# A decoder layer on one core: modulation's third row moved to the vector engine, output projection split in contiguous halves, steps reordered

## The chip, the core and the metric

The kernel runs one hybrid decoder layer in float32 on one core of a Trainium2 chip. The core has a matrix engine (TensorE, in the profile PE, with its weight loads shown apart as PEld), a vector engine (DVE), a scalar engine (ACT), GpSimd (POOL), and SyncE (SP), whose queue here issues nearly all DMAs. The metric is the device time of one execution in microseconds. The kernel before takes 797.26 us, the median of three runs (797.19 to 798.94).

## What is computed

The input is a sequence of 256 tokens with 1024 channels, `x`, and one conditioning vector `c`. Cut to what matters here:

```python
mod = silu(c) @ ada_w + ada_b                      # 6 x 1024 numbers: sh1 sc1 gt1 sh2 sc2 gt2
xn   = rmsnorm(x) * (1 + sc1) + sh1
proj = xn @ w_in                                   # q, kv latent, indexer, rwkv columns, gate_a, gate_r
o_attn = sparse attention (indexer scores, top 64 keys of each query)
o_rwkv = rwkv-7 state recurrence over the sequence
merged = sigmoid(gate_a) * (o_attn @ w_branch_attn) + sigmoid(gate_r) * (o_rwkv @ w_branch_rwkv)
h  = x + gt1 * (merged @ w_out)                    # output projection
xn2 = rmsnorm(h) * (1 + sc2) + sh2
out = h + gt2 * (top-2-of-32 expert SwiGLU MLPs of xn2)
```

All weights, those of all 32 experts included (192 loads of 1 MB), are read from HBM.

## The kernel before, in words

The program has two parts. The front part runs from the first load to the router: modulation, input projection, rwkv, indexer and attention, gates, branches, output projection, router. The second part streams the expert weights through SBUF and multiplies them with the tokens that chose them.

**The modulation.** `ada_w` has 1024 rows and 6144 columns. The kernel treats its result as three rows of 2048 numbers. Row 0 (sh1, sc1) is made first, since everything needs it. Rows 1 and 2 (gt1, sh2, sc2, gt2) are needed only at the output projection and later. They are made by `modulation()`: a row has eight k-parts, each a 1 MB load of 128 by 2048, and `mod_part` (L403 to L407) multiplies it on TensorE: a stationary of 32 columns that all hold the silu of c, and four moving tiles of 512 columns, so that row piece g lands on partitions 32g to 32g+31 of one PSUM bank (line L406). Each float32 matmul leaves two records in the trace, so a k-part has eight.

**Split products.** Products that must be exact use `split` (L510): a 128x512 weight tile w is written as h (w rounded to the engine's short float) and l = w - h, and `mm3` (L528) makes three matmuls, h by x_h, h by x_l, l by x_h (L530, L531, L532). The first letter of a split's code says who makes h (A: ACT at L519, P: POOL at L517), the second who makes l (D: DVE, P: POOL, both at L520). `SPLIT` holds four codes for each stage, taken in turn. There are four pairs of buffers, used round and round.

**The output projection** (L1495 to L1517) works on `w_out` in four loads of two k each. The 1024 output columns are split into eight blocks, and block m takes columns m, m+8, m+16, .... So the split reads the weights with a stride of 8 elements and packs four blocks (128 columns each) into a 128x512 tile; a k has two such tiles, each followed by its 12 matmuls of 128x128 by 128x256. The weight tile that TensorE loads is contiguous.

**The order of the work.** The front part is written as five generators (rwkv, selection, attn, gate, mod), and the string `ORDER` says which of them takes the next step (a letter each). `LORD` gives the order of the weight loads on SP's queue. Loads go into an arena, and are issued as soon as there is room; `RESERVE` holds back part of the arena at each stage. The compiler's scheduler then orders the instructions of an engine; what an engine's row holds at the end is shown below for the places of interest.

Names that the text uses: the X-solve is the 15-step forward substitution of the rwkv chunk (L858 multiply, L859 reduce, on DVE), closed by `diagonal_blocks` (L897, L898) and the copy L905; the latent's norm is an inverse square root in steps of 128x2 on DVE (L360 to L369), and the indexer's small transposes (L1086) and score products (L1101) follow it on TensorE.

Of the kernel before, what the change touches and what calls it, by code (L numbers as in the profile page):

```python
# [57 lines left out]
FORCE0 = True
WIDE = 'a'
_S = ("AD", "PD", "AP", "PD")  # L60
SPLIT = (('PD', 'PD', 'AP', 'AD'), ('PD', 'PD', 'AP', 'PD'), ('PP', 'PP', 'AD', 'AD'), ('AD', 'AP', 'AD', 'AD'), ('AD', 'PD', 'AP', 'PD'))
PRIO = ('mod', 'sel', 'rwkv', 'attn', 'gate')
ORDER = 'rrrrrrmrrmmrrmrrmrrrrrrmrrrmmmrrmrmmmmrsrmaarmrmarrramrmamrrmraarrmmaarmarmaasrmmasaasmmsrarssrasraaarrarrarraasrssasssararasgrssssgraargrsrgsrsgggsrrsmgmmgsmrrrrggrgrgrrggggrsaggrrrggrgrrrgagagaggggaaaagggggaaaggaagggagagggaggaaaaagaggaaaaaggaaaaaaaggaggggggggggg'
LORD = (0, 1, 2, 3, 4, 5, 6, 7, 8, 9, 10, 12, 13, 15, 11, 14, 17, 16, 18, 23, 19, 20, 21, 22, 24, 28, 25, 27, 26, 29, 30, 31, 32, 33, 34, 35, 36, 37, 38, 44, 40, 39, 41, 42, 51, 45, 43, 47, 48, 52, 50, 46, 49)
INFO = []
QUADS = NE // 4
ENDS = ((0, 512), (512, 512))
# [90 lines left out]
def layer_kernel(tc, I, out, dbg=None):  # L158
    nc = tc.nc
    dbg = dbg or (lambda name, ap: None)  # L160
    ALL = CFG[2]
    TOT = ALL - 6144 - 1024 * NP2
    RING = CFG[0] * 4096
    ctxs = []

# [1175 lines left out]

    def modulation():
        rows = []
        i = 0
        for r in (1, 2):
            row = load_adab(r)
            ps = PS()
            for k in range(8):
                yield ("ada", r, k)
                mod_part(ps, r, k, k == 0, k == 7)  # L1350
                if k < 7:
                    yield 1.5
            nc.vector.tensor_add(row, row, ps)
            rows.append(row)
            yield 1.5
# [99 lines left out]
    del pairs[NPO:]  # L1455
# [497 lines left out]
```

## Time and profile before

| | before |
|---|---|
| median of 3 runs | 797.26 us |
| profiled execution | 798.72 us, its span 796.8 us (1.9 outside the span) |
| PE busy | 676.4 us (85%), 4657 instructions |
| DVE / ACT / POOL busy | 285.3 / 167.6 / 144.2 us |
| DMA | 261.38 MB, mean 328 GB/s over the span |
| mean granted TensorE clock | 0.948 of full speed |

The rows of the section further down are whole lines of views of this execution. In a list of groups by line, a row gives line, engine, operation, output<-input (partitions x elements, type), count | busy us, mean ns of one | idle time of the engine ahead of them, and who ended it. In a timeline a row gives start, length, engine, line, operation and count; in brackets stands the idle time before it and who ended it.

### The profile page before, as it was taken

How to read it: one execution, taken by the hardware profiler on the slowest of the kernel's cores; microseconds unless marked ns; L12 is line 12 of the kernel's file. 1: busy time of each engine (PE TensorE's matmuls, PEld its weight loads, DVE VectorE, ACT ScalarE, POOL GpSimd, SP SyncE). 2: the span in 40 equal slices, each digit the busy share in tenths (PEclk: the TensorE clock that was granted, in tenths of full speed). 3: DMA queues.
4: the chain of work that ended last, by engine and by line, in shares of the span. 5: the costliest groups of instructions: out<-in, count | busy, mean ns of one | idle time of the engine just before them, and what ended most of it. 6: DMA issues, size and time to landing. Idle time of an engine off the chain costs nothing.

```text
span 796.8 us, 11470 instructions
## 1 busy us (share of the span) xinstructions
PE 676.4 (85%) x4657; PEld 364.7 (46%) x4657; DVE 285.3 (36%) x665; ACT 167.6 (21%) x347; POOL 144.2 (18%) x176
## 2 busy tenths in 40 slices
PE   5897989799998998889999778878768868878667
PEld 2785657468888877853342312312312312312112
DVE  2577789697336557741210160100100100100001
ACT  2445412144156644321110100100100100000000
POOL 1446744331314117610000000000000000000000
PEclk9899999899999999989999899899999999899889
DMA  9997467443656456779999999999999999999994
GB/s 333 389 308 253 165 221 282 146 154 105 218 208 239 133 178 246 292 257 420 422 421 422 421 420 422 421 420 423 420 421 422 420 421 422 420 421 422 422 392 180
DMA packets 63590, 261.38 MB, mean 328 GB/s; under 512 B 7952, under 2 KB 19216, under 8 KB 38448
## 3 DMA queue, kind: packets, MB, share of 16 engines
q1 hardware_dynamic: 63248, 260.11, 83.4%
q8 instruction: 37, 0.61, 0.3%
q10 hardware_dynamic: 288, 0.52, 0.2%
q14 instruction: 17, 0.14, 0.0%
HBM read 259.57 MB, written 1.05 MB: 327 GB/s over the span
## 4 chain that ended last, share of the span: by engine, by line
DMA 46%; PE 10%; DVE 3%; SPq 1%; issue 1%; POOL 1%; ACT 0%; POOLq 0%; DVEq 0%
DMA arena<-in_expert_w_down_dram 17%; DMA arena<-in_expert_w_gate_dram 13%; DMA arena<-in_expert_w_up_dram 12%; DMA more<-in_expert_w_gate_dram 2%; DMA more<-in_expert_w_up_dram 2%; PE ps_e L1626 2%; DVE split L520 1%; PE ps_e L1611 1%; SPq L288 1%; PE ps_e L1660 1%; PE acc L1701 1%; PE acc L1708 1%; PE ps_e L1653 1%; PE ps_e L1632 0%; PE ps_r L1471 0%
## 5 line engine op out<-in xcount | busy, mean ns | idle before, releaser
L1626 PE MATMUL ps_e<-arena,more 128*32 128x512 f32 x440 | 87.6, 656 | 23.9 <-DMA arena<-in_expert_w_gate_dram 12.0
L1626 PE MATMUL ps_e<-arena 128*32 128x512 f32 x416 | 82.4, 682 | 20.4 <-DMA arena<-in_expert_w_gate_dram 11.7
L1653 PE MATMUL ps_e<-arena 128*32 128x512 f32 x360 | 84.3, 609 | 13.5 <-DMA arena<-in_expert_w_down_dram 9.6
L520 DVE TENSOR_TENSOR split<-arena,split 128x512 fp32r<-128x512 f32 x77 | 70.7, 928 | 45.6 <-ACT split L519 31.8
L1637 ACT ACTIVATE arena<-ps_e 128x512 f32<-128x512 f32 x8 | 4.8, 597 | 244.8 <-PE ps_e L1626 244.8
L1638 DVE SCALAR_TENSOR_TENSOR arena<-arena,ps_e 128x512 f32<-128x512 f32 x8 | 5.5, 688 | 140.2 <-ACT arena L1637 140.2
L1691 POOL TENSOR_TENSOR arena<-arena 128x256 f32<-128x256 f32 x8 | 4.9, 615 | 280.7 <-PE ps_e L1694 279.0
L1670 DVE TENSOR_TENSOR arena<-ps_e,more 128x512 f32<-128x512 f32 (+1 forms) x17 | 11.8, 691 | 122.2 <-PE ps_e L1653 109.1
L519 ACT CAST split<-arena 128x512 fp32r<-128x512 f32 x66 | 45.0, 688 | 48.1 <-PE ps_g L531 30.3
L520 POOL TENSOR_TENSOR split<-arena,split 128x512 fp32r<-128x512 f32 x33 | 47.2, 1431 | 42.6 <-ACT split L519 27.8
L564 PE MATMUL ps_a<-split 128*128 128x256 f32 x360 | 52.1, 304 | 3.1 <-ACT split L476 1.9
L1626 PEld LDWEIGHTS ps_e<-arena,more 128*32 128x32 f32 x440 | 19.4, 118 | 76.3 <-issue 30.9
L564 PEld LDWEIGHTS ps_a<-split 128*128 128x128 f32 x360 | 47.9, 205 | 12.1 <-issue 6.5
L1626 PEld LDWEIGHTS ps_e<-arena 128*32 128x32 f32 x416 | 17.8, 122 | 74.0 <-issue 35.8
L517 POOL TENSOR_SCALAR split<-arena 128x512 fp32r<-128x512 f32 x44 | 36.9, 842 | 70.2 <-PE ps_g L531 18.7
L1653 PEld LDWEIGHTS ps_e<-arena 128*32 128x32 f32 x360 | 19.6, 110 | 64.3 <-issue 31.2
L530 PE MATMUL ps_g<-split 128*128 128x256 f32 x128 | 39.1, 306 | 0.0
L532 PE MATMUL ps_g<-split 128*128 128x256 f32 x128 | 36.9, 289 | 2.0 <-POOL split L520 2.0
L1639 DVE SCALAR_TENSOR_TENSOR arena<-arena,ps_e 128x512 f32<-128x512 f32 x8 | 8.2, 1029 | 82.5 <-PE ps_e L1626 82.5
L531 PE MATMUL ps_g<-split 128*128 128x256 f32 x128 | 36.8, 288 | 0.0
L1611 PEld LDWEIGHTS ps_e<-arena,more 128*128 128x128 f32 x256 | 30.7, 195 | 13.2 <-issue 8.2
L532 PE MATMUL ps_a<-split 128*128 128x256 f32 (+1 forms) x96 | 30.4, 317 | 6.2 <-DVE split L520 6.2
(378 smaller groups left out, 1192.5 us busy)
## 6 DMA issues: line engine op xcount, KB each, us to landing
arena<-in_expert_w_gate_dram SPq DMA_DIRECT2D x54, 1024.0 KB, 19.8
arena<-in_expert_w_up_dram SPq DMA_DIRECT2D x53, 1024.0 KB, 19.8
arena<-in_expert_w_down_dram SPq DMA_DIRECT2D x53, 1024.0 KB, 19.8
arena<-in_w_in_dram SPq DMA_DIRECT2D x18, 1024.0 KB, 7.8
arena<-in_ada_w_dram SPq DMA_DIRECT2D x16, 1024.0 KB, 6.1
more<-in_expert_w_up_dram SPq DMA_DIRECT2D x11, 1024.0 KB, 19.8
more<-in_expert_w_down_dram SPq DMA_DIRECT2D x11, 1024.0 KB, 19.8
arena<-in_ada_w_dram SPq DMA_DIRECT2D x16, 512.0 KB, 10.9
```

Source lines behind the costliest of these rows:

```text
L517: nc.gpsimd.tensor_scalar(h, w, 1.0, 0.0, op0=OP.mult, op1=OP.add)
L519: nc.scalar.copy(h, w)
L520: (nc.gpsimd if p[1] == "P" else nc.vector).tensor_sub(l, w, h.bitcast(F32))
L530: nc.tensor.matmul(ps, l[0], r[0], start=start, stop=False)
L531: nc.tensor.matmul(ps, l[0], r[1], start=False, stop=False)
L532: nc.tensor.matmul(ps, l[1], r[0], start=False, stop=stop)
L564: nc.tensor.matmul(p, a[:, kk, :], b[:, 4 * hf + kk, :], start=(i == 0 and kk == KORD[0]), stop=(i == 2 and kk == KORD[-1]))
L1611: nc.tensor.matmul(ps[:, n * kk:n * kk + n], h2[:, a, 2 * k2 + kk, :], oh(a), start=(a == 0), stop=(a == 1))
L1626: nc.tensor.matmul(ps[32 * g:32 * g + 32, :], xg[:, 4 * i + k, 32 * g:32 * g + 32], w[:, k, :], start=(i == 0 and k == 0), stop=(i == 1 an ...
L1639: nc.vector.scalar_tensor_tensor(hidb[0:r].rearrange("p (j q) -> p q j", j=4), thb[0:r].rearrange("p (q j) -> p q j", j=4), 0.5, psu[0:r, ...
L1653: nc.tensor.matmul(pss[c][32 * g:32 * g + 32, :], hTb[:, 2 * i + j, 32 * g:32 * g + 32], w[:, j, 512 * c:512 * c + 512], start=(i == 0 and ...
L1670: nc.vector.tensor_mul(Yb[0:r, c:c + 512], ps[0:r], gt2[0][0:r, g:g + 512])
```

## The change

Five things change. Line numbers after the first edit fall by one or two.

1. Modulation row 2 (sc2 and gt2) leaves TensorE, but for its last step. A tile `acc` of 128x2048 collects, over the eight k-parts, the weights times the k-th column of silu(c): ACT writes the first, DVE adds the others by scalar_tensor_tensor (four of 128x512 for each k-part). Then four matmuls with a stationary of ones sum over the partitions.
2. The output projection splits contiguous halves of 512 columns into one of two wide buffers (two halves of 1024 columns, in the same memory as the four pairs), and runs the eight blocks of a k once both halves are split. TensorE now takes its stationary tile with a stride of 8 elements. One `SPLIT` code changes there, AP to PP.
3. In stages 1 and 2 the `SPLIT` codes change too: one POOL subtraction goes to DVE, one POOL copy goes to ACT.
4. `ORDER`, `LORD` and `RESERVE` are other tables. Row 2's loads go behind gate, branch and output weights in the load order.
5. The last copies, `leave`, no longer share a tile between DVE and ACT: DVE copies 512 columns.

```diff
-RESERVE = (29696, 12288, 15360, 4096, 0)
+RESERVE = (29696, 16384, 18432, 4096, 0)
-SPLIT = (..., ('PD', 'PD', 'AP', 'PD'), ('PP', 'PP', 'AD', 'AD'), ('AD', 'AP', 'AD', 'AD'), ('AD', 'PD', 'AP', 'PD'))
+SPLIT = (..., ('PD', 'PD', 'AP', 'AD'), ('AP', 'PP', 'AD', 'AD'), ('AD', 'AP', 'AD', 'AD'), ('AD', 'PD', 'PP', 'PD'))
...
-    pairs = [(b.get(512), b.get(512)) for b in [B] * NPO + [B2] * (NP2 - NPO)]
+    wide = [(B.get(1024), B.get(1024)) for _ in range(2)]
+    pairs = [tuple(t[:, 512 * i:512 * i + 512] for t in p) for p in wide for i in range(2)]
...
+        acc = M(2048)
+        for k in range(8):
+            yield ("ada", 2, k)
+            w = need(("ada", 2, k))[:, 0]
+            for q in range(4):
+                s = slice(512 * q, 512 * q + 512)
+                if k == 0:
+                    nc.scalar.mul(acc[:, s], w[:, s], csb[:, k, 0:1])
+                else:
+                    nc.vector.scalar_tensor_tensor(acc[:, s], w[:, s], csb[:, k, 0:1], acc[:, s], op0=OP.mult, op1=OP.add)
+                if q == 1:
+                    yield 0.0, 1.0
+            done(("ada", 2, k))
+            yield 0.0, 1.0
+        row = load_adab(2)
+        ps = PS()
+        for g in range(4):
+            nc.tensor.matmul(ps[32 * g:32 * g + 32, :], ones[:, 0:32], acc[:, 512 * g:512 * g + 512], start=True, stop=True)
+        nc.vector.tensor_add(row, row, ps)
...
-    def out_part(m, k, w, i):
-        mm3(block(m), (w[0][:, i, :], w[1][:, i, :]), (mh[:, k, :], ml[:, k, :]), k == 0 and m > 5,
+    def out_part(m, k, w):
+        mm3(block(m), (w[0][:, m:1024:8], w[1][:, m:1024:8]), (mh[:, k, :], ml[:, k, :]), k == 0 and m > 5,
...
+    cnt_split[0] += cnt_split[0] % 2
     for j in range(4):
         w = need(("wo", j))
-        ws = {}
-        for hh, kk in ((0, 0), (0, 1), (1, 0), (1, 1)) if j == 3 else ((0, 0), (1, 0), (0, 1), (1, 1)):
-            ws[hh, kk] = split(w[:, kk, :].rearrange("p (c k) -> p k c", k=8)[:, 4 * hh:4 * hh + 4, :])
...
+        ws = []
+        for kk in range(2):
+            ws.append(wide[cnt_split[0] // 2 % 2])
+            for hh in range(2):
+                split(w[:, kk:kk + 1, 512 * hh:512 * hh + 512])
+            if j < 3:
+                for m in range(8):
+                    out_part(m, 2 * j + kk, ws[kk])
+                continue
...
-            if a == 0:
-                nc.scalar.copy(y[:, a, c:c + 512], o)
-            else:
-                nc.vector.tensor_copy(y[:, a, c:c + 256], o[:, 0:256])
-                nc.scalar.copy(y[:, a, c + 256:c + 512], o[:, 256:512])
+            (nc.vector.tensor_copy if a else nc.scalar.copy)(y[:, a, c:c + 512], acc[2 * a + c // 512])
```

What the engines' rows look like at three places. First DVE at the end of the X-solve, before: L858 and L859 are the solve's last step, L905, L897 and L898 its closing, L815 a copy of rwkv scores, L520 a split, and L360 the first step of the latent's norm.

```order
177 L858 TENSOR_TENSOR arena<-arena 128x450
178 L520 TENSOR_TENSOR split<-arena,split 128x512
179 L859 TENSOR_REDUCE arena<-arena 128x2x15
180 L905 COPY arena<-arena 128x512
181 L897 STREAM_TRANSPOSE arena<-arena 128x512
182 L898 TENSOR_TENSOR arena<-arena 128x1024
183 L815 TENSOR_SCALAR arena<-ps_r 64x4x64
184 L360 TENSOR_SCALAR arena<-ps_a 128x2
```

The same place on DVE, after: L857 and L858 are now the solve, L896 and L897 the closing, L358 the norm's first step, L360 its second, L363 its third, and L1363 the new additions of row 2.

```order
174 L1363 SCALAR_TENSOR_TENSOR arena<-arena 128x512
175 L858 TENSOR_REDUCE arena<-arena 128x2x13
176 L358 TENSOR_SCALAR arena<-ps_a 128x2
177 L857 TENSOR_TENSOR arena<-arena 128x392
178 L814 TENSOR_SCALAR arena<-ps_r 64x4x64
179 L858 TENSOR_REDUCE arena<-arena 128x2x14
180 L814 TENSOR_SCALAR arena<-ps_r 64x4x64
181 L857 TENSOR_TENSOR arena<-arena 128x450
182 L360 TENSOR_SCALAR arena<-arena 128x2
183 L1086 COPY arena<-ps_a 128x16
184 L858 TENSOR_REDUCE arena<-arena 128x2x15
185 L363 TENSOR_TENSOR arena<-arena 128x2
```

The norm's steps and the indexer's copy now stand within the solve's last steps, ahead of its closing, which stands some 15 rows further down; two additions of row 2 stand within the solve.

Second, DVE after, behind the solve: the additions of row 2 (L1363) among the state's copies (L934), the indexer's score sums (L1108) and the splits (L519).

```order
283 L1363 SCALAR_TENSOR_TENSOR arena<-arena 128x512
284 L1108 SCALAR_TENSOR_TENSOR arena<-arena 128x256
285 L1363 SCALAR_TENSOR_TENSOR arena<-arena 128x512
286 L1108 SCALAR_TENSOR_TENSOR arena<-arena 128x256
287 L1363 SCALAR_TENSOR_TENSOR arena<-arena 128x512 x2
288 L1108 SCALAR_TENSOR_TENSOR arena<-arena 128x256
289 L934 COPY arena<-ps_r 128x256
290 L1108 SCALAR_TENSOR_TENSOR arena<-arena 128x256
291 L519 TENSOR_TENSOR split<-arena,split 128x512
292 L1363 SCALAR_TENSOR_TENSOR arena<-arena 128x512
```

Five additions stand ahead of the split in row 291; in the kernel before none stands there.

Third, POOL in the output projection, before (L517 makes h of a P split, L520 the l of an AP split):

```order
122 L517 TENSOR_SCALAR split<-arena 128x512
123 L520 TENSOR_TENSOR split<-arena,split 128x512
124 L517 TENSOR_SCALAR split<-arena 128x512 x2
125 L520 TENSOR_TENSOR split<-arena,split 128x512
126 L517 TENSOR_SCALAR split<-arena 128x512 x2
127 L520 TENSOR_TENSOR split<-arena,split 128x512
128 L517 TENSOR_SCALAR split<-arena 128x512 x2
```

and after (L516 makes h, L519 the l of the PP split):

```order
112 L516 TENSOR_SCALAR split<-arena 128x512
113 L1322 TENSOR_TENSOR arena<-arena 128x512
114 L516 TENSOR_SCALAR split<-arena 128x512 x3
115 L519 TENSOR_TENSOR split<-arena,split 128x512
116 L516 TENSOR_SCALAR split<-arena 128x512 x3
117 L519 TENSOR_TENSOR split<-arena,split 128x512
118 L516 TENSOR_SCALAR split<-arena 128x512 x3
119 L519 TENSOR_TENSOR split<-arena,split 128x512
```

For two k, POOL had two h and one l, and has three h and one l; the l stands behind both h of its own k.

## Rows read from the trace of the kernel before

**Rows 1.** Chain that ended last, some of its 304 pieces: start, length, what.

```profile
331.56 1.91 DVE split L520
...
387.77 16.59 DMA more<-in_expert_w_up_dram
...
776.18 5.14 PE ps_e L1660 x26
```

**Rows 2.** Busy time by stretch: length, engines, then clock, DMA share, GB/s.

```profile
120.00:140.00 20.00, 18.92 (x223) 14.59 (x221) 18.71 (x50) 5.12 (x11) 8.38 (x13) 1.00 0.80 288
140.00:160.00 20.00, 15.95 (x71) 10.33 (x72) 13.69 (x34) 4.41 (x11) 6.27 (x9) 0.83 0.45 146
...
260.00:280.00 20.00, 19.85 (x160) 17.48 (x159) 11.51 (x34) 11.92 (x31) 4.60 (x5) 1.00 0.39 128
...
360.00:776.00 416.00, 338.86 (x1802) 105.84 (x1798) 51.98 (x106) 25.12 (x57) 5.90 (x9) 0.94 1.01 420
```

**Rows 3.** Groups by line, output projection and router, 300 to 360 us, PE.

```profile
L532 PE MATMUL ps_a<-split 128*128 128x256 f32 x48 | 14.2, 295 | 6.2 <-DVE split L520 6.2
```

**Rows 4.** PE timeline around two k-parts of modulation.

```profile
69.57 1.92 PE L406 MATMUL ps_g<-arena 128*32 128x512 f32 x16
71.42 0.74 PE L564 MATMUL ps_a<-split 128*128 128x256 f32 x4
```

**Rows 5.** Groups by line: DVE's scalar_tensor_tensor on a 128x512 tile.

```profile
L1322 DVE SCALAR_TENSOR_TENSOR arena<-arena,ps_g 128x512 f32<-128x512 f32 x4 | 2.7, 679 | 0.2 <-PE ps_g L532 0.2
```

**Rows 6.** Groups by line, 307 to 335 us, the splitting engines.

```profile
L517 POOL TENSOR_SCALAR split<-arena 128x512 fp32r<-128x512 f32 x8 | 12.5, 1573 | 2.8 <-PE ps_r L531 2.8
...
L520 DVE TENSOR_TENSOR split<-arena,split 128x512 fp32r<-128x512 f32 x12 | 18.7, 1603 | 4.1 <-POOL split L517 4.1
L1325 DVE TENSOR_TENSOR split<-arena,split 128x512 fp32r<-128x512 f32 x3 | 4.2, 1400 | 3.3 <-ACT split L1324 3.3
...
L519 ACT CAST split<-arena 128x512 fp32r<-128x512 f32 x7 | 8.3, 1185 | 7.2 <-PE ps_a L531 7.2
L1324 ACT CAST split<-arena 128x512 fp32r<-128x512 f32 x2 | 1.2, 620 | 8.0 <-DVE arena L1323 5.4 <-POOL arena L1323 2.6
```

**Rows 7.** PE timeline, a wait for a POOL split among gate products.

```profile
246.15 0.39 PE L532 MATMUL ps_g<-split 128*128 128x256 f32 x1 [1.96 <-POOL split L520]
```

**Rows 8.** PE timeline at the end of the X-solve.

```profile
135.55 1.07 PE L406 MATMUL ps_g<-arena 128*32 128x512 f32 x8
...
142.12 0.28 PE L1086 MATMUL ps_a<-arena 8*128 8x8 f32 x2 [2.35 <-DVE arena L360]
...
145.90 0.68 PE L1101 MATMUL ps_a<-arena 32*128 32x128 f32 x4 [1.93 <-DVE arena L365]
...
149.16 0.63 PE L531 MATMUL ps_a<-split 128*128 128x512 f32 x1
...
155.22 0.40 PE L531 MATMUL ps_a<-split 128*128 128x512 f32 x1
```

**Rows 9.** DVE timeline at the same place.

```profile
139.55 1.87 DVE L898 TENSOR_TENSOR arena<-arena 128x1024 f32<-128x1024 f32 x1
...
141.91 0.16 DVE L360 TENSOR_SCALAR arena<-ps_a 128x2 f32<-128x2 f32 x1
```

**Rows 10.** PE timeline, two neighbouring matmuls of the output projection.

```profile
313.10 0.28 PE L530 MATMUL ps_a<-split 128*128 128x256 f32 x1
313.22 0.28 PE L531 MATMUL ps_a<-split 128*128 128x256 f32 x1
```

**Rows 11.** Groups by line, 160 to 300 us, POOL's splits of contiguous tiles.

```profile
L520 POOL TENSOR_TENSOR split<-arena,split 128x512 fp32r<-128x512 f32 x16 | 21.0, 1312 | 26.1 <-ACT split L519 19.4 <-PE ps_a L1235 6.0
L517 POOL TENSOR_SCALAR split<-arena 128x512 fp32r<-128x512 f32 x8 | 5.1, 637 | 19.5 <-PE ps_g L531 18.7 <-PE ps_a L532 0.8
```

**Rows 12.** Weight loads: L1063's with stride 8, and L397's contiguous ones.

```profile
236.92 0.53 PEld L1063 LDWEIGHTS ps_r<-arena 128*128 128x128 f32 x4
...
13.26 0.47 PEld L397 LDWEIGHTS ps_a<-arena 128*128 128x128 f32 x4
```

More of the change, by code (lines that the diff above doesn't have):

```diff
@@ L48 @@
 TMAJ = 0.3
-NP2 = 4
-NPO = 4
 REST = 12.0
@@ L60 @@
 _S = ("AD", "PD", "AP", "PD")
-SPLIT = (('PD', 'PD', 'AP', 'AD'), ('PD', 'PD', 'AP', 'PD'), ('PP', 'PP', 'AD', 'AD'), ('AD', 'AP', 'AD', 'AD'), ('AD', 'PD', 'AP', 'PD'))
+SPLIT = (('PD', 'PD', 'AP', 'AD'), ('PD', 'PD', 'AP', 'AD'), ('AP', 'PP', 'AD', 'AD'), ('AD', 'AP', 'AD', 'AD'), ('AD', 'PD', 'PP', 'PD'))
 PRIO = ('mod', 'sel', 'rwkv', 'attn', 'gate')
-ORDER = 'rrrrrrmrrmmrrmrrmrrrrrrmrrrmmmrrmrmmmmrsrmaarmrmarrramrmamrrmraarrmmaarmarmaasrmmasaasmmsrarssrasraaarrarrarraasrssasssararasgrssssgraargrsrgsrsgggsrrsmgmmgsmrrrrggrgrgrrggggrsaggrrrggrgrrrgagagaggggaaaagggggaaaggaagggagagggaggaaaaagaggaaaaaggaaaaaaaggaggggggggggg'
-LORD = (0, 1, 2, 3, 4, 5, 6, 7, 8, 9, 10, 12, 13, 15, 11, 14, 17, 16, 18, 23, 19, 20, 21, 22, 24, 28, 25, 27, 26, 29, 30, 31, 32, 33, 34, 35, 36, 37, 38, 44, 40, 39, 41, 42, 51, 45, 43, 47, 48, 52, 50, 46, 49)
+ORDER = 'mrrrrrrrrmmrmrrmrrrrrrmrrrrmmmrrmmmmmrrararmmrarrraarrrsraarraararaasrasaassrarssrarrasraarraarrsaasrsasssarraamgrssmsrsgsmaargmrsrgmsrsggmgsrrmggsrrmrrggmrgrsmgrrggmggrsmaggrrmrggamggrgrmrrgamgaggamaggamagggmgaaagmgaagmgggmgagamgaaamagaaggamggaaaaaggaaaaaamgagaggggggggggg'
+LORD = (0, 1, 2, 3, 4, 5, 6, 7, 8, 9, 10, 13, 15, 11, 12, 14, 17, 16, 18, 23, 19, 20, 21, 22, 24, 28, 25, 26, 30, 29, 34, 27, 32, 36, 31, 38, 33, 44, 40, 35, 37, 51, 39, 45, 41, 49, 42, 43, 47, 48, 52, 50, 46)
 INFO = []
@@ L161, in layer_kernel @@
     ALL = CFG[2]
-    TOT = ALL - 6144 - 1024 * NP2
+    TOT = ALL - 10240
     RING = CFG[0] * 4096
@@ L175, in layer_kernel @@
     A = Arena(sb.tile([128, TOT], F32, name="arena"), TOT)
-    nB2 = 2048 + 1024 * (NP2 - NPO)
+    nB2 = 2048
     nB = ALL - TOT - nB2
@@ L1343, in modulation @@
         rows = []
[L1344 to L1355, printed above, removed]
+        row = load_adab(1)
+        ps = PS()
+        for k in range(8):
+            yield ("ada", 1, k)
+            mod_part(ps, 1, k, k == 0, k == 7)
+            if k < 7:
+                yield 1.5
+        nc.vector.tensor_add(row, row, ps)
+        rows.append(row)
+        yield 1.5
+        acc = M(2048)
+        for k in range(8):
+            yield ("ada", 2, k)
[11 more added lines that the diff above has]
+        row = load_adab(2)
+        ps = PS()
+        for g in range(4):
+            nc.tensor.matmul(ps[32 * g:32 * g + 32, :], ones[:, 0:32], acc[:, 512 * g:512 * g + 512], start=True, stop=True)
+        nc.vector.tensor_add(row, row, ps)
+        A.free(acc)
+        rows.append(row)
+        yield 0.9
         A.free(cs, csb)
@@ L1454, in layer_kernel @@
     state["stage"] = 4
-    del pairs[NPO:]
     fr2.__exit__(None, None, None)
@@ L1487, in block @@
         return pso[m // 2][:, 256 * (m % 2):256 * (m % 2) + 256] if m < 6 else pso[m - 3][:, 0:256]
-    def out_part(m, k, w, i):
-        mm3(block(m), (w[0][:, i, :], w[1][:, i, :]), (mh[:, k, :], ml[:, k, :]), k == 0 and m > 5,
+    def out_part(m, k, w):
+        mm3(block(m), (w[0][:, m:1024:8], w[1][:, m:1024:8]), (mh[:, k, :], ml[:, k, :]), k == 0 and m > 5,
             k == 7 and m not in (0, 2, 4))
+    cnt_split[0] += cnt_split[0] % 2
     for j in range(4):
         w = need(("wo", j))
-        ws = {}
-        for hh, kk in ((0, 0), (0, 1), (1, 0), (1, 1)) if j == 3 else ((0, 0), (1, 0), (0, 1), (1, 1)):
-            ws[hh, kk] = split(w[:, kk, :].rearrange("p (c k) -> p k c", k=8)[:, 4 * hh:4 * hh + 4, :])
-            for i in range(4 if j < 3 else 0):
-                out_part(4 * hh + i, 2 * j + kk, ws[hh, kk], i)
-            for m in range(4 * hh, 4 * hh + 4 if j == 3 and kk else 0):
+        ws = []
[7 more added lines that the diff above has]
+                continue
+            for m in range(8 if kk else 0):
                 for k2 in range(2):
-                    out_part(m, 6 + k2, ws[hh, k2], m % 4)
+                    out_part(m, 6 + k2, ws[k2])
                 for n in {3: (0,), 4: (1,), 5: (2,), 6: (3,), 7: (4, 5)}.get(m, ()):
@@ L1786, in leave @@
         for a in range(2):
-            o = acc[2 * a + c // 512]
-            if a == 0:
-                nc.scalar.copy(y[:, a, c:c + 512], o)
-            else:
-                nc.vector.tensor_copy(y[:, a, c:c + 256], o[:, 0:256])
-                nc.scalar.copy(y[:, a, c + 256:c + 512], o[:, 256:512])
+            (nc.vector.tensor_copy if a else nc.scalar.copy)(y[:, a, c:c + 512], acc[2 * a + c // 512])
             (nc.scalar if a else nc.sync).dma_start(out=out[0, 128 * a:128 * a + 128, c:c + 512], in_=y[:, a, c:c + 512])
```

## The prediction

> **What bounds the kernel now.** I read the chain that ended last first, from its end backwards. It ends in matmuls behind the last expert load (776.18); from 387.77 up to there nearly every piece is an expert load, and ahead of that it is front work, the splits of the output projection among it [rows 1]. Between 360 and 776 us the DMA share is 1.01 at 420 GB/s, while PE is busy 339 of 416 us [rows 2]. So nothing done to the engines inside the stream moves the end. What moves it is when the stream starts in earnest: its loads are issued as the front part gives buffers back, and the share of loads ahead of the output projection stays as it was. An earlier end of the front (the last piece of the output projection in the chain starts at 331.56, [rows 1]) goes to the end one for one.
>
> The table by stretch then says what bounds the front. PE is busy 18.9 of 20 us at 120 to 140 and 19.9 at 260 to 280 at full clock, DVE 11.5 in the latter [rows 2]: there work taken from PE is time. At 120 to 140 DVE too is busy, 18.7 of 20, and at 140 to 160 neither is full (16.0 and 13.7) and the clock is 0.83 [rows 2]: there it is a chain of dependent steps. In the output projection PE waits 6.2 us for the splits of DVE [rows 3].
>
> **Row 2 of modulation.** Two k-parts hold PE from 69.57 to 71.42 [rows 4], so one takes 0.93 us. Eight go, 7.4 us; the four new matmuls have the records of one k-part, so 0.9 comes back: 6.5 us less on PE. Five of the eight stood between 117 and 147 us (one is the row at 135.55 [rows 8]), where DVE is as busy as PE [rows 2] and PE also waits; the three others stood later, among products without gaps. If only these three count, 3 x 0.93 - 0.93 = 1.9 us is left; if all do, 6.5. PE is busy 95% of 120 to 140, and the new order pulls other products up there, so I take 5.5.
>
> On DVE, seven k-parts of four additions are 28 instructions. The nearest row, the same operation at the same size, is 0.679 us [rows 5]: 28 x 0.68 = 19.0 us. (Next to a busy POOL a DVE operation of this size took 1.40 [rows 6], so the other end is 39 us.) Two stand inside the X-solve, the others behind it, where DVE has 8 of 20 us free [rows 2]. The cover is that free time; what is queued behind an addition is a split that PE waits for. Where five stand ahead of one split, it is late by up to 3.4 us. PE's own queue of other products covers some of it: the row that shows such a miss is one wait of 1.96 us for a split [rows 7]. If none of the 28 shows, 0; if a third of them does, 9 x 0.68 = 6.1. I take 2.6, four splits late by one addition each beyond their slack: 4 x 0.68 = 2.7, less the rounding.
>
> **The norm of the latent ahead of the solve's closing.** In the kernel before PE waits 2.35 us for the norm's first step and 1.93 for a later one [rows 8]. DVE did that step at 141.91, 0.16 us long, only behind the solve's closing, whose last product took 1.87 [rows 9]. After these waits the clock is at its lower level for about 6.5 us: a product of 512 columns takes 0.63 there and 0.40 behind it [rows 8], so about 3.2 us of those are lost. Together 2.35 + 1.93 + 3.2 = 7.5 us. In the new order the norm's steps stand inside the solve's last steps, so the waits as such should go; but the closing comes later by two additions, the norm and the score sums (about 3 us), and the rwkv chain that needs it waits instead. Bounds: 3 us worse to 7.5 better. I take 2.0 better, since PE then needs other work to fill with and has five k-parts less of it.
>
> **Output projection.** A matmul starts every 0.12 us [rows 10]; 192 of them make 23 us, and a k (24) takes 2.9. Reading with a stride, POOL takes 1.57 for h, DVE 1.60 for l, ACT 1.19 for h [rows 6]; on contiguous tiles POOL takes 0.64 for h and 1.31 for l [rows 11], ACT 0.62, and DVE 1.40 even beside POOL [rows 6]. For a k with AD and PD the new chain is 0.64, then two subtractions on DVE one behind the other: 0.64 + 2 x 1.40 = 3.4 with POOL beside it, 0.64 + 2 x 0.68 = 2.0 without. For a k with PP and PD, POOL makes both h and then l: 0.64 + 0.64 + 1.31 = 2.6. With two wide buffers a k's splits may take as long as the k before is multiplied, 2.9 us. So most of the 6.2 us goes; what is late next is the start, since no product of a k can begin with half its columns (one more split, about 1 us), and some 0.4 us in the DVE pairs, four times. 6.2 - 1.0 - 1.6 = 3.6, and I take 3.0; bounds 0 to 6. The POOL code that goes from AP to PP costs nothing here by the same 2.6 against 2.9; without that cover 0.4 a k.
>
> The one new thing on PE is a stationary tile with a stride of 8. The trace has one such load, the indexer's transposes: four in 0.53 us, against 0.47 for four contiguous loads [rows 12]. That is 0.015 us a load, 192 x 0.015 = 2.9 us if none of it is hidden; the loads lie beside matmuls that start every 0.12, and 0.53/4 is 0.13 with the overlap at the end still in it, so I cost it at nothing. [...]
>
> **The rest.** SPLIT of stages 1 and 2, POOL l to DVE or POOL h to ACT: 0.6 us less on POOL, as much more on ACT, which is busy 4.4 to 11.9 of 20 [rows 2]; nothing, within 1 us either way. Row 2's loads move behind other weights; they are used late, and the DMA share at 140 to 160 is 0.45 and at 260 to 280 0.39 [rows 2], so there is room; but by the new order the second half of one gate's weights and the last branch load get their buffers late, with other loads queued on SP ahead of them. Nothing if in time; at worst a wait like the longest in these rows, some 2 to 3 us [rows 8]. The last copies: 0.1 us.
>
> **Sum.** -5.5 - 2.0 - 3.0 - 0.1 + 2.6 = -8.0 us. Made in the profiled execution (798.72 us, its span 796.8), it gives 790.7; that execution is 1.46 above the median, so on the median of 797.26 it is 789.3.
>
> **Rivals.**
> 1. DVE becomes the bound. 19 us of additions sit ahead of splits, and each PE wait of some length is followed by a stretch at the lower clock (as behind the waits of [rows 8]). For: DVE is busy 18.7 of 20 where the first additions go. Against: behind 200 us it has 8 of 20 free. Price: 6 us of waits and 3 of clock instead of 2.6: 797.3 - 8.0 + 6.4 = 795.7, no change or barely faster.
> 2. The chain behind the solve gives all: waits and clock stretch of 139 to 155 go in full, and so do 6.5 of PE and 4 of the projection: 797.3 - 6.5 - 7.5 - 4 + 2 = 781.3. For: in the new rows of DVE the norm stands ahead. Against: less filling work.
> 3. Strided weight loads slow the projection. ACT's strided read is 1.19/0.62 = 1.9 times its contiguous one; if a load's spacing grows likewise, 0.12 to 0.23, 192 x 0.11 = 21 us come on top: 797.3 - 5.0 + 21 = 813. It decides against the change from a spacing of 0.12 + 8/192 = 0.16 on. Against: [rows 12]. [...]
> 4. The solve's closing is late. It moves behind the norm and score sums on a DVE that is full; the rwkv chain starts later by 3 us, PE runs out of products there since five k-parts are gone, waits 5 us more and falls to the lower clock for a stretch of 6.5 (3.2 lost); with splits late by 6 that outdoes the 9: 797.3 - 8.5 + 8.2 + 6 = 803. It decides when waits and clock cost over 8.
>
> **How the numbers follow.** Forecast 0.52, with its own range 783.5 to 794.5 (its terms' bounds that don't fall to a rival). Rival 1 0.16, rival 2 0.12, rival 3 0.06, rival 4 0.14. A measurement can't tell less than about 0.3% (2.4 us) from no change. Faster: all of forecast and rival 2 and a third of rival 1, 0.69; same: 0.13, two thirds of rival 1 and a little of 4; slower: 0.18. The range that leaves out 2 in 10 is 780 to 801.
>
> **What would show it.** In the changed profile: L404 with 64 records fewer; 28 additions near 0.68 us; PE's waits in 139 to 146 gone and the clock there at its upper level; PE waits on DVE's split in the projection under 3.5 us; matmul spacing there still 0.12 (above 0.16 rival 3 holds); the last split of the projection starting near 324 us; the last expert load landing about 8 us ahead of 776. Splits behind the additions that hold PE for over 5 us in all between the solve and the branches, or a last split after 331, would make it wrong.

## The result: 1.4% slower, and the profile after

The changed kernel takes 809.0 us (808.2 to 810.7) beside 798.1 for the kernel before in the same round: a ratio of 1.014, interval 1.0123 to 1.0157. Faster by 8 us was forecast. The profiled execution takes 809.25 us, its span is 807.5, 10.7 longer than before.

The chain that ended last has the same form as [rows 1]: the expert stream, bound by its loads, takes over ten microseconds later (start, length, what):

```profile
397.72 16.83 DMA more<-in_expert_w_up_dram
```

Before, that piece began at 387.77, 10 us earlier. So the loss is in the front part, and two rows of the PE timeline bracket the place. The first is the first product of the output projection (307.63 before), the second the row sums behind its last (343.12 before):

```profile
301.77 0.51 PE L529 MATMUL ps_a<-split 128*128 128x256 f32 x1 [0.83 <-POOL split L516]
...
352.48 1.71 PE L1496 MATMUL ps_r<-arena 128*128 128x1 f32 x12
```

The projection starts 5.9 us earlier and lasts 50.7 us instead of 35.5, 15.2 longer. -5.9 + 15.2 is 9.3, nearly the whole loss. Its products come next. These rows, from the groups by line from 290 to 365 us, are to be held against [rows 3]; they have 144 of the 192 products, the other 48 write `ps_r`:

```profile
L529 PE MATMUL ps_a<-split 128*128 128x256 f32 x48 | 19.5, 406 | 0.8 <-POOL split L516 0.8
L530 PE MATMUL ps_a<-split 128*128 128x256 f32 x48 | 19.4, 405 | 0.0
L531 PE MATMUL ps_a<-split 128*128 128x256 f32 x48 | 19.4, 408 | 0.0
```

The waits for DVE's splits are gone, 6.2 us of them. The 0.8 us for POOL that is left lies ahead of the first product. But a product has a mean of 406 ns where it had about 290. The timeline, to be held against [rows 10], shows what that does to the spacing, and the weight loads beside it:

```profile
302.85 0.41 PE L529 MATMUL ps_a<-split 128*128 128x256 f32 x1
303.09 0.40 PE L530 MATMUL ps_a<-split 128*128 128x256 f32 x1
303.33 0.41 PE L531 MATMUL ps_a<-split 128*128 128x256 f32 x1
```

```profile
302.96 0.34 PEld L530 LDWEIGHTS ps_a<-split 128*128 128x128 f32 x1
303.20 0.34 PEld L531 LDWEIGHTS ps_a<-split 128*128 128x128 f32 x1
```

Products start every 0.24 us and not every 0.12, and a load takes 0.34 instead of 0.19. The clock is not the reason: in the stretches of the projection (length, PE, PEld, DVE, ACT, POOL, granted clock, DMA share, GB/s) it is at its upper level, and PE is full (the slices from 340 to 352 us are at 1.00 as well):

```profile
300.00:320.00 20.00, 19.16 (x83) 18.78 (x82) 9.69 (x12) 2.38 (x4) 7.93 (x9) 1.00 0.84 331
320.00:340.00 20.00, 20.00 (x85) 20.00 (x84) 6.11 (x6) 1.24 (x2) 5.68 (x8) 1.00 0.24 76
```

The sum of this one term is 192 x 0.12 = 23 us. The 6.2 us of waits come off it, which gives 16.8; where the 1.6 us between that and the measured 15.2 lie was not traced.

### The profile page after: what moved, and what is told of

Its sections match the earlier page's. It is cut to its first block, busy times and chain, and to the rows that moved or that the text cites. A ratio compares the mean times of both kernels' runs of the same rounds, so it can differ in the third digit from the quotient of the medians.

```text
span 807.5 us, 11382 instructions
## 1 busy us (share of the span) xinstructions
PE 685.5 (85%) x4601; PEld 385.6 (48%) x4601; DVE 298.1 (37%) x693; ACT 167.9 (21%) x354; POOL 133.0 (16%) x171
## 3 DMA queue, kind: packets, MB, share of 16 engines
HBM read 259.57 MB, written 1.05 MB: 323 GB/s over the span
## 4 chain that ended last, share of the span: by engine, by line
DMA 48%; PE 13%; DVE 1%; POOL 1%; ACT 0%; issue 0%; SPq 0%; POOLq 0%
DMA arena<-in_expert_w_down_dram 14%; DMA arena<-in_expert_w_up_dram 12%; DMA arena<-in_expert_w_gate_dram 12%; DMA more<-in_expert_w_up_dram 5%; DMA more<-in_expert_w_gate_dram 2%; DMA more<-in_expert_w_down_dram 2%; PE ps_e L1650 2%; PE ps_a L531 1%; PE ps_a L529 1%; PE ps_a L530 1%; PE ps_e L1635 1%; PE acc L1725 1%; PE ps_e L1677 1%; PE ps_r L529 0%; PE ps_r L530 0%; PE ps_r L531 0%
## 5 line engine op out<-in xcount | busy, mean ns | idle before, releaser
L1650 PE MATMUL ps_e<-arena 128*32 128x512 f32 x808 | 167.7, 667 | 41.5 <-DMA arena<-in_expert_w_up_dram 20.9
L1650 PEld LDWEIGHTS ps_e<-arena 128*32 128x32 f32 x808 | 36.6, 119 | 139.6 <-issue 58.8
L1677 PE MATMUL ps_e<-arena 128*32 128x512 f32 x344 | 81.0, 615 | 12.5 <-DMA arena<-in_expert_w_down_dram 8.6
L1650 PE MATMUL ps_e<-more,arena 128*32 128x512 f32 x184 | 78.6, 684 | 12.3 <-DMA more<-in_expert_w_gate_dram 6.2
L519 DVE TENSOR_TENSOR split<-arena,split 128x512 fp32r<-128x512 f32 x77 | 64.2, 841 | 47.2 <-POOL split L516 27.2
L518 ACT CAST split<-arena 128x512 fp32r<-128x512 f32 x71 | 43.3, 618 | 77.3 <-PE ps_r L530 27.5
L519 POOL TENSOR_TENSOR split<-arena,split 128x512 fp32r<-128x512 f32 x33 | 44.7, 1355 | 66.5 <-ACT split L518 56.1
L1694 DVE TENSOR_TENSOR arena<-ps_e,arena 128x512 f32<-128x512 f32 (+1 forms) x17 | 11.8, 691 | 114.2 <-PE ps_e L1677 101.7
L1677 PEld LDWEIGHTS ps_e<-arena 128*32 128x32 f32 x344 | 19.3, 111 | 61.4 <-issue 30.8
L516 POOL TENSOR_SCALAR split<-arena 128x512 fp32r<-128x512 f32 x39 | 28.3, 730 | 63.9 <-PE ps_r L530 19.8
L529 PE MATMUL ps_g<-split 128*128 128x256 f32 x128 | 38.2, 298 | 0.0
L531 PE MATMUL ps_g<-split 128*128 128x256 f32 x128 | 36.2, 283 | 1.9 <-POOL split L519 1.9
L529 PE MATMUL ps_a<-split 128*128 128x256 f32 (+1 forms) x96 | 36.3, 380 | 0.8 <-POOL split L516 0.8
L1677 PE MATMUL ps_e<-more,arena 128*32 128x512 f32 x104 | 34.3, 612 | 3.1 <-DMA more<-in_expert_w_down_dram 1.6
L530 PE MATMUL ps_a<-split 128*128 128x256 f32 (+1 forms) x96 | 35.5, 370 | 1.3 <-DVE split L519 1.3
```

What stands on the lines that cost most here:

```text
L516: nc.gpsimd.tensor_scalar(h, w, 1.0, 0.0, op0=OP.mult, op1=OP.add)
L518: nc.scalar.copy(h, w)
L519: (nc.gpsimd if p[1] == "P" else nc.vector).tensor_sub(l, w, h.bitcast(F32))
L529: nc.tensor.matmul(ps, l[0], r[0], start=start, stop=False)
L530: nc.tensor.matmul(ps, l[0], r[1], start=False, stop=False)
L531: nc.tensor.matmul(ps, l[1], r[0], start=False, stop=stop)
```

## The experiments

Theory S: the stationary tile with stride 8 is what costs, and the rest of the change is a gain. Rivals: that the new order left something in front of the projection (F), or that the wide buffers, and not the stride, slow the loads (B). Each ratio is against the kernel before timed in the same round: 797.2 us for e1 to e3, 798.0 for e5 to e8, 797.5 for e9. A difference in us between two rounds carries up to 0.8 us of that.

**The projection put back in the changed kernel** (`e1_old_projection`).

```diff
-        mm3(block(m), (w[0][:, m:1024:8], w[1][:, m:1024:8]), ...
+        mm3(block(m), (w[0][:, i, :], w[1][:, i, :]), ...
...
-                split(w[:, kk:kk + 1, 512 * hh:512 * hh + 512])
+            ws[hh, kk] = split(w[:, kk, :].rearrange("p (c k) -> p k c", k=8)[:, 4 * hh:4 * hh + 4, :])
```

> The changed kernel with the output projection of the kernel before (splits read with stride 8, stationary tiles contiguous, codes AD PD AP PD). Theory S (a strided stationary tile costs twice the spacing, 0.241 against 0.12 us, and all else of the change is a gain): the projection starts 5.9 us earlier than before, as in the changed kernel, and lasts as long as before, so about 797.5 - 6 = 791 to 792 us, spacing 0.12. Rival F (the projection is slow because of what the new order and loads left in front of it): near 809 us, spacing above 0.2.

Measured: 792.6 us, ratio 0.9943 (0.9921 to 0.9965). Theory S holds; F falls. The products are back at [rows 3], with its waits, and start every 0.12 us again:

```profile
L531 PE MATMUL ps_a<-split 128*128 128x256 f32 x48 | 14.2, 295 | 6.3 <-DVE split L519 6.3
```

```profile
311.77 0.28 PE L529 MATMUL ps_a<-split 128*128 128x256 f32 x1
311.89 0.28 PE L530 MATMUL ps_a<-split 128*128 128x256 f32 x1
```

**The new projection alone in the kernel before** (`e2_new_projection_in_before`), the same edit the other way round.

> The kernel before with only the output projection changed (contiguous splits in wide buffers, stationary tiles with stride 8, codes AD PD PP PD). Theory S: 192 matmuls x 0.121 us = 23 us more on PE, about 8 of it back from waits and an earlier first split, so 811 to 814 us. Rival F: 794 to 798 us, spacing 0.12.

Measured: 813.9 us, ratio 1.0214 (1.0196 to 1.0233). By itself the new projection costs 2.1%, some 17 us; the rest of the change had hidden a third of it.

**Contiguous stationary tiles in the same wide buffers** (`e3_permuted_write`).

```diff
-        mm3(block(m), (w[0][:, m:1024:8], w[1][:, m:1024:8]), ...
+        mm3(block(m), (w[0][:, 128 * m:128 * m + 128], w[1][:, 128 * m:128 * m + 128]), ...
...
+        h, l = (t.rearrange("p (m c) -> p c m", m=8)[:, 64 * hh:64 * hh + 64, :] for t in wide[...])
```

> The changed kernel, but the splits write the columns in block order (contiguous reads, stride of 128 elements in the writes of h and l), so that the stationary tiles are contiguous in the same wide buffers. Theory S: spacing back to 0.12, the splits pay for their strided writes (1 to 2 us each), 790 to 797 us. Rival B (not the stride but the wide buffers, written in one half while the other is loaded, slow the weight loads): spacing stays near 0.24 and 805 to 812 us.

Measured: 799.2 us, 1.0024 (1.0009 to 1.0039), above what S expected, below what B did. The loads decide between them: 205 ns, not 337, in the same buffers. So B falls, and the price moved to the splits, whose strided writes make PE wait 10.4 us:

```profile
L1522 DVE TENSOR_TENSOR split<-arena,split 128x512 fp32r<-128x512 f32 x12 | 18.1, 1532 | 11.0 <-POOL split L1519 11.0
...
L531 PE MATMUL ps_a<-split 128*128 128x256 f32 x48 | 15.0, 315 | 10.4 <-DVE split L1522 10.4
...
L530 PEld LDWEIGHTS ps_a<-split 128*128 128x128 f32 x48 | 9.9, 205 | 0.0
```

The longest of these waits, 4.99 us up to 312.65, is followed by a stretch at the lower clock, 0.50 from 311 to 316 us, where products start every 0.21 to 0.22 us; at 305 and at 326 us, at 1.00, they start every 0.12. That too is in the 799.2 us:

```profile
313.67 0.41 PE L529 MATMUL ps_a<-split 128*128 128x256 f32 x1
313.89 0.41 PE L530 MATMUL ps_a<-split 128*128 128x256 f32 x1
```

**The loads by themselves** (`e4_weight_loads`), streams of matmuls with nothing beside them.

> Not the layer: a kernel that loads x and runs streams of 32 matmuls (64 in the first), stationary 128x128, moving 256 columns unless said, and nothing beside them, then copies PSUM out. Streams in order: type of the splits with stride 1, 2, 4, 8, and 8 with 512 columns moving; bf16 with stride 1, 4, 8; plain float32 with stride 1 and 8; transposes of float32 (128 columns) with stride 1 and 8; the splits' type with 128 columns moving and stride 1 and 8. Theory S: in the splits' type stride 8 has a spacing of 0.24 against 0.12 for stride 1, stride 4 or 2 lies between or is free; with 512 columns moving the load hides (0.23 a matmul). For the transposes the layer's trace showed 0.11 at stride 8, so they stay equal. Rival B: all strides of one type have one spacing.

The PE timeline has a row for each stream; the distance of two starts over 32 is the spacing. First the splits' type: stride 1, 2, 4, 8, then 8 with 512 columns moving:

```profile
16.19 4.00 PE L102 MATMUL ps<-xr 128*128 128x256 f32 x32
20.03 4.00 PE L104 MATMUL ps<-xr 128*128 128x256 f32 x32
23.87 7.64 PE L106 MATMUL ps<-xr 128*128 128x256 f32 x32
31.34 7.87 PE L108 MATMUL ps<-xr 128*128 128x256 f32 x32
39.04 8.13 PE L110 MATMUL ps<-xr 128*128 128x512 f32 x32
47.01 3.67 PE L112 MATMUL ps<-xb 128*128 128x256 bf16 x32
```

That is 0.120, 0.120, 0.233, 0.241 and 0.249 us: stride 2 is free, stride 4 and 8 double the spacing, and a product of 512 moving columns takes about that long itself (in the kernel before, at a granted clock of 1.00, such products start at 154.98, 155.22 and 155.45 us, every 0.23 to 0.24), so the load of 331 ns adds some 0.01. Then the transposes of plain float32, contiguous and with stride 8, and behind them the splits' type with 128 columns moving, contiguous and with stride 8. The loads of the transposes follow (ns: least, median, most):

```profile
86.61 3.66 PE L122 MATMUL ps<-ident,xin 128*128 128x128 f32 x32
90.10 3.75 PE L124 MATMUL ps<-ident,xin 128*128 128x128 f32 x32
93.61 3.77 PE L126 MATMUL ps<-xr 128*128 128x128 f32 x32
97.21 7.88 PE L128 MATMUL ps<-xr 128*128 128x128 f32 x32
```

```profile
L122 PEld LDWEIGHTS ps<-ident,xin x32: 139/140/163, 86.4 to 89.9; 128*128 128x128 f32 x32
...
L124 PEld LDWEIGHTS ps<-ident,xin x32: 188/193/197, 90.0 to 93.5; 128*128 128x128 f32 x32
```

The transposes are at 0.109 and 0.110: equal in spacing. The load is longer, by 53 ns, and lies hidden. This is what deceived the prediction. The splits' type with half the moving columns is at 0.1125 ((97.21 - 93.61)/32), hardly below the 0.120 of 256 columns, which points to the contiguous load (192 ns in both) as the bound there. Products of plain float32 with 256 columns, two records each, go from 0.432 to 0.478 us with stride 8.

**More strides, and the moving tile** (`e10_strides`).

> Not the layer: streams of 32 matmuls as in e4_weight_loads, in the splits' type, 256 columns moving: stationary stride 1 (64, then 32), 2, 3, 4, 6; then stationary contiguous and the moving tile with stride 2, 4, 8; then bf16 with 64 columns moving, stationary stride 8 and 1. [...] For the moving tile: 0.12 if the stream of columns is read at half the need, else up to 0.24. bf16 at 64 columns: a visible cost of stride 8, if its longer load (143 against 98 ns) was only hidden by 256 columns.

Stationary stride 2, 3, 4, 6, then a contiguous one with the moving tile at stride 2, 4 and 8; and bf16 with 64 columns moving, stationary stride 8 and then 1:

```profile
19.93 4.00 PE L104 MATMUL ps<-xr 128*128 128x256 f32 x32
23.77 5.78 PE L106 MATMUL ps<-xr 128*128 128x256 f32 x32
29.38 7.63 PE L108 MATMUL ps<-xr 128*128 128x256 f32 x32
36.85 7.46 PE L110 MATMUL ps<-xr 128*128 128x256 f32 x32
44.14 7.52 PE L112 MATMUL ps<-xr 128*128 128x256 f32 x32
51.48 7.64 PE L114 MATMUL ps<-xr 128*128 128x256 f32 x32
58.95 7.17 PE L116 MATMUL ps<-xr 128*128 128x256 f32 x32
```

```profile
65.94 2.12 PE L118 MATMUL ps<-xb 128*128 128x64 bf16 x32
67.90 1.10 PE L120 MATMUL ps<-xb 128*128 128x64 bf16 x32
68.83 1.17 PE L123 MATMUL ps<-xr 128*128 128x512 f32 x4
```

Stationary: 0.120, 0.175, 0.233, 0.228. So the spacing does not grow further from stride 4 to 6. The moving tile differs: at stride 2 it takes 0.229 already, and 0.233 and 0.218 at 4 and 8. bf16 with stride 8 takes 0.061 against 0.029 (loads of 157 and 99 ns), which 256 columns had hidden in e4 (0.110, 0.109 and 0.109 at stride 1, 4 and 8). Why the cost sets in between stride 2 and 4 for the stationary tile, and at 2 for the moving one, no run shows.

The length of a load's record and the spacing go together. Where the load sets the pace, the spacing is 80 to 96 ns less than the record: 192 ns and 0.1125 us (128 columns, contiguous), 262 and 0.175 (stride 3), 329 and 0.233 (stride 4), 337 and 0.241 (stride 8). By this estimate the strided load of a transpose (193 ns) needs 0.10 to 0.11 us, no more than the transposes take anyway.

**A stride that costs nothing on both sides** (`e5_pairs`). If stride 2 is free for the load, the splits may keep pairs of columns together and read runs of two.

```diff
-            ws[hh, kk] = split(w[:, kk, :].rearrange("p (c k) -> p k c", k=8)[:, 4 * hh:4 * hh + 4, :])
+            ws[hh, kk] = split_pairs(w[:, kk, :].rearrange("p (c a b) -> p a c b", a=4, b=2)[:, 2 * hh:2 * hh + 2])
...
-        mm3(block(m), (w[0][:, i, :], w[1][:, i, :]), ...
+        mm3(block(m), tuple(t[:, i // 2, i % 2::2] for t in w), ...
```

> e1_old_projection with splits that read runs of two neighbouring columns (stride 8 between the runs) and keep the pairs, so that the stationary tile has stride 2. Theory S, with the streams of e4_weight_loads (stride 2 costs 0.120 us, as stride 1): spacing 0.12, splits shorter than with single elements (between 0.7 and 1.6 us), waits of PE on DVE's split below the 6.3 us of e1, so 787 to 791 us against 792.6. Rival B (any stride in the stationary tile costs in the layer): spacing above 0.15 and over 797 us. Rival N (pairs read no faster than single elements): splits at 1.2 to 1.6 us as in e1, 792 to 793 us.

Measured: 786.1 us, ratio 0.9857 (0.9839 to 0.9875), faster than both kernels. The loads keep 195 ns and the products start every 0.12 us (311.76, 311.88, 312.00); the splits on DVE fall from 1612 ns (in e1) to 912, where those of contiguous halves take 955 in the changed kernel, and the wait falls from 6.3 us to 1.1:

```profile
L531 PE MATMUL ps_a<-split 128*128 128x256 f32 x48 | 13.8, 287 | 1.1 <-DVE split L1518 1.1
L1518 DVE TENSOR_TENSOR split<-arena,split 128x512 fp32r<-128x512 f32 x12 | 10.7, 912 | 5.1 <-POOL split L1515 4.3 <-PE ps_a L530 0.6
...
L531 PEld LDWEIGHTS ps_a<-split 128*128 128x128 f32 x48 | 9.4, 195 | 1.5 <-DVE split L1518 1.5
```

**The same in the kernel before** (`e7_pairs_in_before`).

> The kernel before with the splits in pairs and stationary tiles of stride 2, nothing else. Theory S: the 6.2 us of waits in the projection fall to 2 to 4, 792 to 795 us. Rival N: 797 us. Rival B: over 802 us.

Measured: 790.0 us, 0.9913 (0.9885 to 0.9941), a little better than expected. The shorter splits that the change was after are worth about 1% here, once TensorE doesn't pay for them. PE's wait for them falls from 6.2 us to 1.1; why the time falls by some 2 us more was not traced.

**What row 2's additions cost** (`e6_few_additions`).

```diff
-                else:
+                elif q == 3:
+                    s = slice(2032, 2048)
                     nc.vector.scalar_tensor_tensor(acc[:, s], w[:, s], csb[:, k, 0:1], acc[:, s], ...)
```

> e1_old_projection with most of row 2 left out: of the 28 additions on DVE seven are left, one for each k-part, with 16 columns instead of 512; loads, order and the four matmuls stay. It tells what the additions cost beside the splits. By the prediction's term (2.6 us) it is at 790 us against 792.6; if the additions hide wholly, 792 to 793; if they hold DVE where PE waits for it, 785 to 787.

Measured: 787.9 us, 0.9878 (0.9861 to 0.9895), 4.7 us below e1 (5.2 by the ratios). The additions cost more than the 2.6 us of the prediction. Two of PE's waits in e1, 1.28 us for a split of DVE at 160.59 and 2.09 us for a DVE step of the state at 202.96, are absent from e6. One reason stands in e1's groups by line, 130 to 290 us, DVE: a mean of 893 ns, where 679 was taken from [rows 5]:

```profile
L1363 DVE SCALAR_TENSOR_TENSOR arena<-arena 128x512 f32<-128x512 f32 x28 | 24.6, 893 | 1.1 <-DMA arena<-in_ada_w_dram 1.1
```

Another is where they stand. The prediction read 8 of 20 us free on DVE from the stretch at 260 to 280 us, but the additions of the changed kernel start between 136.6 and 249.6. In its profile DVE (the third of the engines) is all but full there, where it was at 13.69, 17.97 and 14.80 in the kernel before:

```profile
140.00:160.00 20.00, 19.32 (x147) 13.50 (x146) 19.14 (x50) 9.27 (x22) 6.11 (x7) 1.00 0.18 54
160.00:180.00 20.00, 17.80 (x234) 12.11 (x233) 19.63 (x67) 9.31 (x15) 4.49 (x6) 1.00 0.80 263
180.00:200.00 20.00, 20.00 (x240) 18.19 (x240) 19.09 (x48) 8.32 (x16) 5.54 (x8) 1.00 0.54 182
```

**What PE work is worth there** (`e8_extra_kparts`): eight unused k-parts beside the additions.

```diff
+            ps = PS()
+            for g in range(4):
+                nc.tensor.matmul(ps[32 * g:32 * g + 32, :], csb[:, k, :], w[:, 512 * g:512 * g + 512], start=True, stop=True)
             done(("ada", 2, k))
```

> e1_old_projection with eight k-parts put back on TensorE at the places where row 2's last additions stand (their result is not used, so row 2 is made on DVE as well). It tells what 7.4 us of PE work are worth there. If the front is bound by PE at these places, as the prediction's term has it (5.5 of 6.5): 6 to 8 us more than e1, 799 to 800 us. If PE has slack there: 793 to 795.

Measured: 795.4 us, 0.9977 (0.9961 to 0.9993), 2.8 us above e1 (2.7 by the ratios), a difference whose size is loose, since the two intervals touch (e1 0.9921 to 0.9965). It is nearer to slack than to a full price. Part of the k-parts fell into waits: ahead of the projection PE waits 16.8 us (from 40 us on) where it waits 21.6 in e1, and the wait of 2.09 us at 202.96 is not in its timeline.

**Row 2 on TensorE at the new places** (`e9_row2_by_kpart`), made from e5.

```diff
-                    nc.vector.scalar_tensor_tensor(acc[:, s], w[:, s], csb[:, k, 0:1], acc[:, s], op0=OP.mult, op1=OP.add)
+                nc.tensor.matmul(ps[32 * g:32 * g + 32, :], csb[:, k, :], w[:, 512 * g:512 * g + 512], start=True, stop=True)
...
+                nc.vector.tensor_add(row, row, ps)
```

> e5_pairs with row 2 back on TensorE at the late places: each k-part is four matmuls of its own, and DVE adds its 128x512 result to the row (7 additions and the bias instead of 28 and the bias; the 128x2048 tile goes). Seen so far against e1: leaving out nearly all additions 4.7 us less, eight extra k-parts 2.8 us more. If the two add up: 786.1 - 4.7 x 20/28 + 2.8 = 785.5, no difference that can be told from e5. If moving row 2 to DVE was a gain by itself, as the prediction had it (5.5 of PE against 2.6 of waits): 789 us. If the additions were the dearer part: 782 to 784.

Measured: 792.8 us, 0.9948 (0.9929 to 0.9967), 6.7 us above e5 (7.3 by the ratios). So row 2 on DVE is a gain, as predicted, and larger. It doesn't fit the two prices before: added up, e6 and e8 let no difference be expected. Its projection starts at 306.3 us, e5's at 300.3, with 17.8 us of PE waits ahead against 19.4 (40 us on). So the k-parts of e9 took up 1.6 us of waits, those of e8 4.8. One reason is a new wait, for the DVE addition of a k-part's result (L1366):

```profile
197.59 0.39 PE L529 MATMUL ps_g<-split 128*128 128x256 f32 x1 [1.99 <-DVE arena L1366]
```

Whether that is the whole of why k-parts cost 6.7 here and 2.8 in e8 stays open.

## Why the prediction was wrong

1. **Failed: the stationary tile with stride 8, "so I cost it at nothing".** It cost 0.12 us for each of 192 matmuls, 23 us, in a stretch where PE was full; the projection got 15.2 us longer after the 6.2 us of waits came off, and putting it back (e1) gave back 16.4. The bound of 2.9 us beside it was wrong too. It came from [rows 12], the one strided load of the trace. The difference of those two rows, 0.53 - 0.47 = 0.06 us, is the extra length of the last load alone (192 - 140 ns), and not four times 0.015. And the row was no like case: a transpose of plain float32, whose contiguous load takes 140 ns, where the splits' takes 190. In the one the longer load still hides below the spacing (e4: 0.109 and 0.110); in the other the contiguous load is already at the edge (0.1125 with 128 columns moving, against 0.120 with 256), and stride 8 passes it. The trace before showed it, in a column that I had left for the spacing: the loads' own length, 192 with the stride and 140 without (ns: least, median, most):

```profile
L1063 PEld LDWEIGHTS ps_r<-arena x16: 188/192/208, 234.7 to 240.1; 128*128 128x128 f32 x16
```

```profile
L397 PEld LDWEIGHTS ps_r<-arena x12: 138/140/145, 11.9 to 13.1; 128*128 128x128 f32 x12
```

   The third rival named this mechanism, its sign (a spacing above 0.16), the spacing itself (0.23, measured 0.24) and a price of 21 us (23). It had a chance of 0.06, and its time, 813, was 4 us off. Its price came from ACT's strided read, so its closeness is in part luck. A row that was unlike in type, in mode and in what it lay beside was taken as a measurement against it.
2. **Right: the projection's waits go.** 6.2 us to none within the projection, about the upper bound. But PE was now slow enough to hide these splits, so this doesn't test the term. e5 shows what shorter splits are worth with PE at its old pace, about 6.5 us (792.6 to 786.1; 7 by the ratios), more than the 3.0 taken.
3. **Right in sum, in part by luck: the front gains.** Row 2, the norm and the additions were put at -5.5 - 2.0 + 2.6 = -4.9 us; the projection starts 5.9 us earlier, and e1 is 0.57% faster. Two misses of size offset each other. The additions cost 4.7 and not 2.6 (e6): this is rival 1's mechanism, DVE full where the additions stand, at a part of its price. And moving row 2 as a whole gives 6.7 where 2.9 net was expected (e9). The groups by line from 60 to 300 us, before and then after, show why: the products of modulation take 9.8 us less of PE (19.5 against 8.6 + 1.1), where 6.5 at most was read from two k-parts of 0.93 us. Some 2 us of the difference are two k-parts of row 2 that stood in two pieces before, each piece as long as a whole k-part: two records took 1.04 us from 142.92 and six 1.06 from 146.51, two 1.05 from 200.88 and six 1.06 from 203.48, where eight took 1.07 at 135.55 [rows 8], all at a granted clock of 1.00.

```profile
L406 PE MATMUL ps_g<-arena 128*32 128x512 f32 x128 | 19.5, 629 | 0.0
```

```profile
L404 PE MATMUL ps_g<-arena 128*32 128x512 f32 x64 | 8.6, 633 | 0.0
L1371 PE MATMUL ps_g<-arena 128*32 128x512 f32 x8 | 1.1, 604 | 0.0
```

4. **Right and wrong: the norm ahead of the closing.** The waits of [rows 8] are gone but for 0.68 us at 144.49, but others stand earlier and later in the changed kernel's PE timeline, for DVE steps of the rwkv chain:

```profile
127.89 1.79 PE L797 MATMUL ps_r<-arena 64*64 64x128 f32 x16 [2.69 <-DVE arena L814]
...
203.71 0.27 PE L952 MATMUL ps_r<-arena 64*64 64x64 f32 x1 [2.09 <-DVE arena L981]
```

   The first stands ahead of the first addition (136.6 us) and of the solve's end, so it is not theirs (the new order and the codes of stages 1 and 2 were not taken apart); PE's waits at this line (L797) are 8.0 us in all, all before 130 us, and were 3.9. The second is absent from e6, so it comes with the additions. From 40 us to the projection PE waits 22.0 us, where it waited 16.8 before. So 5.9 us earlier with 5.2 us more of waits is some 11 us less of PE's own time, of which modulation's 9.8 above are the most.

   The stretch at the lower clock moved and did not go: the granted clock is 1.00 at 140 to 160 us, where it was 0.83, but 0.91 at 120 to 140, where it was 1.00, and its mean from 40 us to the projection is 0.97 in both. So nothing shows the 3.2 us that the term's upper bound had from the clock:

```profile
120.00:140.00 20.00, 16.78 (x202) 15.23 (x200) 16.70 (x47) 7.46 (x15) 8.42 (x10) 0.91 0.28 93
```

   Nor did a stretch at the lower clock follow each longer wait, as rival 1 had it: behind the 2.69 us at 127.89 the granted clock is 0.53 (128 to 130 us), but behind the 2.09 us at 203.71 it is 1.00 (203 to 209), and so it was in the kernel before behind the 2.09 us up to 316.66 in the projection (316 to 320).

   How much the norm's place alone is worth was not measured. Rival 4 (PE starved behind a late closing) had its condition, since the closing's last product starts at 148.91 and not at 139.55 ([rows 9]), 9 us later where 3 were expected; but none of the longer waits above is for it: the first stands ahead of it, and the second comes with the additions.
5. **Not contradicted:** loads that come later, the codes of stages 1 and 2 and the last copies. PE waits for no load between 130 us and the projection; DVE waits 1.8 us in two waits for loads of row 2. No run takes these terms apart. Both codes that change in stages 1 and 2 (PD to AD, PP to AP) move a POOL copy to ACT; no subtraction goes to DVE.

## What to carry to other kernels

Before a stationary tile is read with a stride, hold the length of its weight load, for the same type and mode, against the spacing of its matmuls. The loads overlap, so the record may be longer than the spacing (192 ns at 0.120 us in e4); in the streams here a load had no cover left once its record less some 0.08 to 0.10 us came up to the spacing. Where columns must be interleaved, share the stride out: runs of two elements for the engines that copy (912 ns a split on DVE in e5, against 1612 with single ones in e1), stride 2 for the stationary tile (0.120 us a product in e4; 786.1 us here, against 797 and 809). And a wait that vanishes is a gain only if the engine that waited did not become slower. Free time of an engine is to be read from the stretch where the new work will stand.

## What the runs showed of the hardware

- In the splits' type, stationary stride 1 and 2: 0.120 us a matmul of 256 columns; stride 3: 0.175; 4 and 6: 0.23; 8: 0.24. With 512 columns moving, stride 8 takes 0.249, hidden but for some 0.01 us (e4, e10).
- The moving tile already pays at stride 2, where the stationary tile costs nothing (0.120): 0.229 us ((51.48 - 44.14)/32); stride 4 takes 0.233 and stride 8 0.218 (e10).
- The strided load did not slow down with TensorE's clock: in e4's last stream (stride 8, 128 columns moving) 22 loads run from 99.2 to 104.2 us at a granted clock of 0.50, and 22 in the 5 us from 31.4 at 1.00 (stride 8, 256 columns); the median record is 337 ns in both streams.
- The granted clock stayed at its upper level, 1.00, in the long projection, where PE and its loads were busy all the time (20.00 of 20 us each from 320 to 340) and a product started every 0.24 us.
